# A mixture-of-experts layer: 64 of 256 tokens by gathered rows on VectorE, the down tiles as plain fp32 products, no weight table

## The chip, the core and the metric

One core of a Trainium2 chip runs the whole program in one launch. The metric is the device time in microseconds, from the first to the last work of the program. One execution with the hardware profiler on gives the trace.

## The reference

One decoder layer on 256 tokens of 1024 features: a mixing part (retention and sparse attention) and then PEER, a mixture of 16384 single-neuron experts, in which each token picks 16 experts in each of 8 heads. The change is in the PEER part:

```python
q = (hblk @ w_q).reshape(B, TB, PEER_HEADS, 2, PEER_DHALF)
s = jnp.einsum('btphd,phnd->btphn', q, subkeys).astype(jnp.float32)
v, i = lax.top_k(s, PEER_TOPK)
cand = (v[..., 0, :, None] + v[..., 1, None, :]).reshape(B, TB, PEER_HEADS, PEER_TOPK * PEER_TOPK)
cidx = (i[..., 0, :, None] * PEER_NKEYS + i[..., 1, None, :]).reshape(...)
tv, tj = lax.top_k(cand, PEER_TOPK)
eidx = jnp.take_along_axis(cidx, tj, axis=-1)
w = jax.nn.softmax(tv, axis=-1)
u = w_down[eidx]
a = jax.nn.gelu(jnp.einsum('btd,btpkd->btpk', hblk, u).astype(jnp.float32))
vv = w_up[eidx]
return jnp.einsum('btpk,btpkd->btd', (w * a).astype(hblk.dtype), vv)
```

After it come a gated residual add and a final RMSNorm. `w_down` and `w_up` are 16384 x 1024 in float32, 64 MB each.

## The kernel before

**Stages.** Up to 182 us runs the part before PEER ("prefix"). Then a list of units is worked off in order: 16 `wq` units (the query products, 512 KB of weights each), 128 `down` units and 128 `up` units. A unit takes one tile of 128 experts, 512 KB, all 256 tokens at once, so all 16384 experts are computed densely. Down tile n: the 256 tokens' h2 times 128 rows of `w_down`, then Gelu, kept as a 128 x 256 tile of V (tiles 0 to 63 in `VL`, the others in `VH`). Up tile j: V's tile j times 128 rows of `w_up`, added up in four banks of PSUM (`acc_o[tt][hf]`: two halves of the tokens, two halves of the features). V holds Gelu values times routing weights, and these are zero for the experts that a token did not pick.

**How a product is made.** TensorE takes float32 in a fast form, fp32r, that keeps fewer bits. So every streamed tile `raw` is split into a high part `H` (ScalarE, a copy into fp32r) and a rest `L` (VectorE, raw minus H), and a product is three: high x high, rest x high, high x rest (`mm3`). In the rows, `hH,H`, `hL,H` and `hH,L` are those of a down tile (8 chunks of 128 features x 3 = 24 products of 256 columns), and `H,a`, `L,a`, `H,a` those of an up tile (4 banks x 3 = 12 products of 512 columns), where `a` is V's tile split the same way (`a1`, `a2`).

**Selection.** Beside the wq units and the first downs, VectorE picks the top 16 of each half and head (`top_gen`). The generator is stepped by a credit per unit (`CQ`, `CT`), each step naming its price.

**Routing weights.** They are put in place in two ways. Tokens 0 to 127 by one-hots (`w_gen`): for 4 tokens at a time VectorE and ScalarE make one-hot matrices of the two halves of the expert numbers (`o`, `ow`, f16), and 8 small products give the 128 x 128 weights of each token, which are multiplied into V (or copied there, and the Gelu multiplied in later as `g`). This makes 32 groups between down units, one for each unit at the price `CD`. Tokens 128 to 255 by a table in DRAM, `wd`: GpSimd writes zeros into it (8 transfers of 1 MB), then adds the weights with 128 scattered transfers (`put_weights`, line 1009), and each up unit loads its 128 x 128 part `wt2` (64 KB, in the rows `wt<-wd`), which VectorE multiplies into V's tile in `up_units`.

**Order of units.** Ups begin when `w_gen` is done and `START_UP` units have passed: then the downs that are left alternate with ups, and the rest are ups alone. Tiles are loaded on SP's queue `PRE = 4` units ahead, into `RAW = 3` raw buffers; the split of a unit is issued one unit ahead (`SPL`), with `HB = LB = 4` buffers. Each engine works off its own queue of instructions in order. `gate_unit` (8 products of 128 x 1024 on VectorE with the gate's weights `wadaT`) is put to every fourth up from `GATE`. The last three up units are one block, in which a bank is finished before the next is begun, and the tail (gate, residual, norm, store) follows.

Of the kernel before, what the change touches and what calls it, by code (L numbers as in the profile page):

```python
# [24 lines left out]
F32 = mybir.dt.float32  # L25
# [11 lines left out]
P = 128  # L37
T = 256
# [13 lines left out]
GATE = 28  # L52
# [5 lines left out]
ZC = 2048  # L58
START_UP = 108
# [6 lines left out]
def build(tc, I, out, dbg=None, stop=None):  # L66
# [60 lines left out]
    wd2 = mk(dpool, (NT * P, P), F32, "wd")  # L127
    wd = wd2.rearrange("a (b o) -> (a b) o", o=1)
# [13 lines left out]
    def split(key, n=None):  # L142
# [3 lines left out]
        S.activation(h[:, :n], r[:, :n], AF.Copy)  # L146
# [43 lines left out]

    pre = ExitStack()
# [116 lines left out]
    hH = mk(pers, (P, KC, T), F32R, "hH")  # L308
    hL = mk(pers, (P, KC, T), F32R, "hL")
# [83 lines left out]
    dump("hT", f(hH))  # L393
# [401 lines left out]
    h2H = mk(pers, (P, KC, T), F32R, "hH")  # L795
    h2L = mk(pers, (P, KC, T), F32R, "hL")
    ss2 = mk(pp, (P, 2, 3), F32, "ss2")
    shift = [mod[:, 3 * KC + k:3 * KC + k + 1] for k in range(KC)]
    for tt in range(2):
# [26 lines left out]
        for hf, b in enumerate(bs):  # L826
# [8 lines left out]
            for q in range(4):  # L835
# [12 lines left out]
    if stop == "prefix":  # L848
        Q.dma_start(out[0:P, :], f(h2H).rearrange("p a b -> p (a b)")[:, :D])
        psp["es"].close()  # L850
        es.close()
        return

# [75 lines left out]
    def top_gen(sc):  # L929
# [8 lines left out]
        for tt in (1, 0):  # L938
# [40 lines left out]
            if tt:  # L979
                continue  # L980
# [386 lines left out]
```

## Time and profile before

| | |
|---|---|
| Median of 3 runs | 1027.58 us (1026.66 to 1028.56) |
| The profiled execution | 1026.25 us |
| Its span, first to last instruction | 1024.4 us |
| TensorE / VectorE / ScalarE / GpSimd busy | 990.2 / 742.9 / 558.2 / 271.1 us |
| Mean granted TensorE clock | 0.993 |
| First wq product / start of the last matmul | 182.05 / 1013.56 us |
| Wq units | 182 to 236 us |
| Downs with selection beside them | 236 to 386 us |
| 32 weight groups between downs | 386 to 526 us |
| Downs alone | 526 to 590 us |
| 16 pairs of a down and an up | 590 to 682.7 us |
| 109 ups alone | 682.7 to 1003 us |
| Last three ups, then the tail | to 1013.9 us, to 1024.4 us |

An engine's busy time is the union of its instructions. Matmuls overlap in the rows (a product of 256 columns shows 0.28 us, but the next starts 0.12 us later), so the price of a product is read from one start to the next. A wait stands in the "idle before" column of a group, with what released it. In the rows an operation stands at the line of a helper, L82, so they are told apart by tile.

### The profile page before, as it was taken

What the parts mean: (1) busy time and instruction counts of PE and PEld (TensorE: products, weight loads), DVE (VectorE), ACT (ScalarE), POOL (GpSimd) and SP (SyncE); (2) the same over time, 40 slices, a digit from 0 to 9 for tenths busy, and PEclk for the clock granted to TensorE, in tenths of its full rate; (3) what the DMA queues carried; (4) which work ended last, traced back from release to release, by engine and by line L of the source; (5) the groups of instructions that cost most, each with busy time, mean ns of one, the idle gap of its engine ahead of it and who ended that gap; (6) DMA issues with size and microseconds to landing.
All of it is one profiled execution on the core that took longest, in us unless ns stands there. A gap on an engine that the chain in (4) does not pass through costs nothing. (4 is left out here: it accounts for less than half of the span.)

```text
span 1024.4 us, 17290 instructions
## 1 busy us (share of the span) xinstructions
PE 990.2 (97%) x6323; PEld 870.8 (85%) x6323; DVE 742.9 (73%) x1647; ACT 558.2 (54%) x1077; POOL 271.1 (26%) x175
## 2 busy tenths in 40 slices
PE   7999999999999999999999999999999989999995
PEld 6876678999999999999999979988877668777773
DVE  7987988899999997667755455656666656655656
ACT  7544984455544548777754454554444445444443
POOL 1040000200087787787778600000000000000001
PEclk9999999999999999999999999999999999999998
DMA  9979654975577776666676567766778776666662
GB/s 367 409 298 342 209 196 128 356 297 181 175 181 188 183 178 153 142 146 142 139 157 184 134 211 208 206 203 195 251 242 252 244 246 208 200 201 201 205 194 81
DMA packets 94196, 216.00 MB, mean 211 GB/s; under 512 B 27912, under 2 KB 44576, under 8 KB 92704
## 3 DMA queue, kind: packets, MB, share of 16 engines
q1 hardware_dynamic: 73632, 201.99, 61.2%
q0 software_dynamic: 20336, 12.66, 7.6%
q8 instruction: 49, 0.80, 0.3%
q14 instruction: 35, 0.29, 0.1%
q10 hardware_dynamic: 144, 0.26, 0.1%
HBM read 204.31 MB, written 10.56 MB: 210 GB/s over the span
## 5 line engine op out<-in xcount | busy, mean ns | idle before, releaser
L82 ACT ACTIVATE H<-raw 128x1024 fp32r<-128x1024 f32 x284 | 300.2, 1059 | 246.9 <-DMA raw<-in_up_dram 138.2
L82 DVE TENSOR_TENSOR L<-raw,H 128x1024 fp32r<-128x1024 f32 x284 | 346.0, 1219 | 57.1 <-ACT H L82 53.4
L82 PE MATMUL acc<-H,a 128*128 128x512 f32 (+1 forms) x1030 | 325.4, 394 | 8.9 <-DVE a L82 5.7
L1009 POOL DMA_INDIRECT wd<-VL x128 | 241.0, 1883 | 151.1 <-DVE VL L82 95.9
L82 PEld LDWEIGHTS acc<-H,a 128*128 128x128 f32 x1030 | 190.9, 189 | 56.0 <-DVE a L82 10.6
L82 PE MATMUL acc<-L,a 128*128 128x512 f32 (+1 forms) x515 | 203.4, 395 | 6.1 <-DVE L L82 5.7
L82 PE MATMUL acc<-hH,H 128*128 128x256 f32 x704 | 201.8, 287 | 0.0
L82 PE MATMUL acc<-hL,H 128*128 128x256 f32 x704 | 199.6, 284 | 0.0
L82 PE MATMUL acc<-hH,L 128*128 128x256 f32 x704 | 199.2, 283 | 0.0
L82 PEld LDWEIGHTS acc<-hL,H 128*128 128x128 f32 x704 | 134.6, 191 | 0.2 <-DVE hL L82 0.2
L82 PEld LDWEIGHTS acc<-hH,H 128*128 128x128 f32 x704 | 134.6, 192 | 0.0
L82 PEld LDWEIGHTS acc<-hH,L 128*128 128x128 f32 x704 | 134.5, 191 | 0.0
L82 PE MATMUL dn<-hH,H 128*128 128x256 f32 x448 | 127.6, 285 | 0.0
L82 PE MATMUL dn<-hH,L 128*128 128x256 f32 x448 | 126.8, 283 | 0.6 <-DVE L L82 0.6
L82 PE MATMUL dn<-hL,H 128*128 128x256 f32 x448 | 126.8, 283 | 0.0
L82 PEld LDWEIGHTS acc<-L,a 128*128 128x128 f32 x515 | 97.1, 188 | 33.8 <-DVE L L82 14.7
L82 PEld LDWEIGHTS dn<-hH,H 128*128 128x128 f32 x448 | 85.8, 191 | 0.6
L82 PEld LDWEIGHTS dn<-hH,L 128*128 128x128 f32 x448 | 85.6, 191 | 0.8 <-DVE L L82 0.8
L82 PEld LDWEIGHTS dn<-hL,H 128*128 128x128 f32 x448 | 85.6, 191 | 0.6
L82 DVE TENSOR_TENSOR VL<-VL,wt 128x128 f32<-128x128 f32 x64 | 18.6, 291 | 85.5 <-DMA wt<-wd 85.5
L82 DVE TENSOR_TENSOR VH<-VH,wt 128x128 f32<-128x128 f32 x64 | 18.7, 292 | 74.4 <-DMA wt<-wd 74.4
L82 ACT ACTIVATE ow<-o,VL 128x128 f16<-128x128 f16 x128 | 52.4, 578 | 0.0
(345 smaller groups left out, 1212.5 us busy)
## 6 DMA issues: line engine op xcount, KB each, us to landing
raw<-in_down_dram SPq DMA_DIRECT2D x128, 512.0 KB, 3.8
raw<-in_up_dram SPq DMA_DIRECT2D x128, 512.0 KB, 4.0
adaraw<-in_wadaT_dram SPq DMA_DIRECT2D x40, 512.0 KB, 7.0
raw<-in_wq_dram SPq DMA_DIRECT2D x16, 512.0 KB, 8.3
wd<-VL POOLq DMA_DIRECT2D x8, 1024.0 KB, 18.2
wt<-wd SPq DMA_DIRECT2D x128, 64.0 KB, 3.3
raw<-in_win_C_dram SPq DMA_DIRECT2D x12, 512.0 KB, 7.4
rawA<-in_win_A_dram SPq DMA_DIRECT2D x8, 512.0 KB
```

The source lines that it names most:

```text
L82: i = fn(*a, **kw)
L1009: i = G.indirect_dma_start(wd, bass.IndirectOffsetOnAxis(ap=eid[:, p, k:k + 1], axis=0), exd[:, p, k:k + 1], None, compute_op=ALU.add)
```

## The change

The tokens are divided anew: 64 sparse ones (`TS`, tokens 0 to 63) and 192 dense ones (`TD`).

- The sparse tokens go without dense tiles. Each has 128 picked experts; two tokens' lists lie over the 128 partitions in halves (`idxS`, `wS`: partition p is token p of the first 64 slots, partition 64 + p the same token's other 64). 64 gathers of 128 rows of `downN` (512 KB each, on GpSimd's queue) bring the rows, and VectorE multiplies each with the token's own h2 (`h2rep`) and sums over the features into a column of `dotS`; Gelu and weight give `cS`; then 64 gathers of rows of `up` follow, which VectorE adds up, scaled, into `accS`. The rows have `BD + 1 = 4` buffers. A step (one gathered tile) is issued by a credit of 0.7 for each down and 0.45 for each up unit.
- The dense down tiles are plain fp32 products of the raw tile with `h2f` (192 columns), 8 a tile, with no split.
- The up tiles take 10 products instead of 12: the 64 dense tokens of the first half go as 128 columns, high and rest side by side, with two products for each half of the features; the other 128 tokens as before. `a` is made one unit ahead (`prepare`).
- All 192 dense tokens get their weights by one-hots (48 groups); table, zeroing, scattered additions and `wt2` are gone. Ups begin as soon as the groups are done.
- The halves of the packed columns and of `accS` are brought together in the last block by 8 products with a matrix `sel`.
- `RAW` is 4, `HB` and `LB` 3. The gate's weights are loaded one gate step earlier.

The diff, cut to its core:

```diff
-RAW = 3
-HB = 4
-LB = 4
+RAW = 4
+HB = 3
+LB = 3
-GATE = 28
+GATE = 36
+TS = 64
+TD = T - TS
+NJ = P // 2
+BLK = 8
+BD = 3
+RD = 0.7
+RU = 0.45
-START_UP = 108
...
+    for hf in range(2):
+        b = bank("S")
+        for q in range(4):
+            k = hf * 4 + q
+            for n, a in enumerate((h2H, h2L)):
+                mm(b[:, q * P:(q + 1) * P], a[:, k, :P], identR, n == 0, n == 1)
+        S.activation(h2rep[:TS, hf * 512:(hf + 1) * 512], b[:TS, :], AF.Copy)
+    G.dma_start(h2rep[TS:, :], h2rep[:TS, :])
+    for n in range(2):
+        G.tensor_tensor(h2f[:, 4 * n:4 * n + 4, :], h2[n][:, :, 0, TS:].bitcast(F32), h2[n][:, :, 1, TS:].bitcast(F32),
+                        op=ALU.add)
...
+    def gather(tag, src, j, bufs):
+        r = mk(sp, (P, D), F32, tag, bufs=bufs)
+        G.indirect_dma_start(r, None, src, bass.IndirectOffsetOnAxis(ap=idxS[:, j:j + 1], axis=0))
+        return r
...
+        get_d(BD)
+        yield
+        for j in range(NJ):
+            r = rowD.pop(j)
+            V.scalar_tensor_tensor(r, r, 1.0, h2rep, op0=ALU.mult, op1=ALU.mult, accum_out=dotS[:, j:j + 1])
+            get_d(j + 1 + BD)
+            if j + 1 + BD > NJ:
+                get_u(j + 1 + BD - NJ)
+            if j % BLK == BLK - 1:
+                js = slice(j + 1 - BLK, j + 1)
+                S.activation(cS[:, js], dotS[:, js], AF.Gelu_apprx_tanh)
+                V.tensor_tensor(cS[:, js], cS[:, js], wS[:, js], op=ALU.mult)
+            yield
+        for j in range(NJ):
+            V.scalar_tensor_tensor(accS, rowU.pop(j), cS[:, j:j + 1], accS, op0=ALU.mult, op1=ALU.add)
+            get_u(j + 1 + BD)
+            yield
...
     def down_unit(n):
-        h, l = splits.pop(("down", n))
+        r, _ = raws.pop(("down", n))
...
-            mm3(b, h[:, ks], l[:, ks], h2H[:, k, :], h2L[:, k, :], k == 0, k == KC - 1)
+            mm(b, r[:, k * P:(k + 1) * P], h2f[:, k, :], k == 0, k == KC - 1)
...
+    def prepare(j, ap):
...
+            a = mk(ap, (P, TD, 2), F32R, "a", bufs=3)
+            S.activation(a[:, :, 0], v, AF.Copy)
+            last["U"] = V.tensor_tensor(a[:, :, 1], v, f(a[:, :, 0]), op=ALU.subtract)
...
     def up_units(js, ap):
...
-            V.tensor_tensor(v[:, P:], v[:, P:], wts.pop(j), op=ALU.mult)
...
+                        if tt:
+                            pr = ((a[:, TS:, 0], h), (a[:, TS:, 0], l), (a[:, TS:, 1], h))
+                        else:
+                            a0 = a[:, :TS, :].rearrange("p a b -> p (a b)")
+                            pr = ((a0, h), (a0, l))
...
+        if spg:
+            scred += RU if u == "up" else RD
+            while scred >= 1.0 and spg:
+                scred -= 1.0
+                with tc.issue_after(last["U"].ins):
+                    if next(spg[0], StopIteration) is StopIteration:
+                        spg.pop()
```

On TensorE, before, the end of a down tile and the first up tile behind it (`dn` and `acc` are PSUM banks; 24 rows of the first kind make a tile, 12 of the second):

```order
L82 MATMUL dn_7689<-hH_1712,H_7650 128x256
L82 MATMUL dn_7689<-hL_1713,H_7650 128x256
L82 MATMUL dn_7689<-hH_1712,L_7651 128x256
L82 MATMUL acc_7570<-H_7685,a_1357_7727 128x512
L82 MATMUL acc_7570<-L_7686,a_1357_7727 128x512
L82 MATMUL acc_7570<-H_7685,a_1358_7728 128x512
L82 MATMUL acc_7571<-H_7685,a_1357_7727 128x512
L82 MATMUL acc_7571<-L_7686,a_1357_7727 128x512
L82 MATMUL acc_7571<-H_7685,a_1358_7728 128x512
```

After, the last downs alone and the first up tile; a row with x8 is a whole down tile:

```order
L87 MATMUL dn_5885<-h2f_1960,raw_5799 128x192 x8
L87 MATMUL acc_5822<-H_5881,a_5899 128x512
L87 MATMUL acc_5822<-L_5882,a_5899 128x512
L87 MATMUL acc_5823<-H_5881,a_5899 128x512
L87 MATMUL acc_5823<-L_5882,a_5899 128x512
L87 MATMUL acc_5824<-H_5881,a_5899 128x512
L87 MATMUL acc_5824<-L_5882,a_5899 128x512
L87 MATMUL acc_5824<-H_5881,a_5899 128x512
L87 MATMUL acc_5825<-H_5881,a_5899 128x512
L87 MATMUL acc_5825<-L_5882,a_5899 128x512
L87 MATMUL acc_5825<-H_5881,a_5899 128x512
```

A down tile has become 8 products of 192 columns with the raw tile itself as the stationary one, and each of the first two banks of an up tile has lost its third product.

On VectorE, before, in the middle of the ups alone:

```order
L82 TENSOR_TENSOR a_1614_9023<-VL_1953,a_1613_9022 128x256
L82 TENSOR_TENSOR VL_1953<-VL_1953,wt_1598_8959 128x128
L82 TENSOR_TENSOR L_9018<-raw_8932,H_9017 128x1024
L82 TENSOR_TENSOR a_1620_9048<-VL_1953,a_1619_9047 128x256
L82 TENSOR_TENSOR VL_1953<-VL_1953,wt_1604_8984 128x128
L82 TENSOR_TENSOR L_9043<-raw_8957,H_9042 128x1024
L82 TENSOR_TENSOR a_1626_9073<-VL_1953,a_1625_9072 128x256
```

After, at a like place:

```order
L87 SCALAR_TENSOR_TENSOR accS_2003<-row_8147,cS_2002,accS_2003 128x1024
L87 TENSOR_TENSOR L_8275<-raw_8209,H_8274 128x1024
L87 TENSOR_TENSOR a_8278<-VH_3713,a_8278 128x192
L87 TENSOR_TENSOR L_8294<-raw_8231,H_8293 128x1024
L87 TENSOR_TENSOR a_8297<-VH_3713,a_8297 128x192
L87 TENSOR_TENSOR L_8313<-raw_8250,H_8312 128x1024
L87 TENSOR_TENSOR a_8316<-VH_3713,a_8316 128x192
L87 SCALAR_TENSOR_TENSOR accS_2003<-row_8188,cS_2002,accS_2003 128x1024
```

The product with `wt` is gone, `a` has 192 columns instead of 256, and a step of `accS` stands behind every second or third tile.

On GpSimd, before, from the spill of x2 on:

```order
L842 DMA x2d_71<-xn_92 128x2048
L877 DMA subT_1960<-in_subT_dram 128x2048
L878 IOTA ioi_1961 128x512
L879 IOTA tok_1962 128x1
L884 MEMSET VL_1953 128x2048
L886 DMA wd_74<-VL_1953 128x2048 x8
L1009 DMA wd_74<-VL_1953 2097152x1 x128
```

After, from the same place (a row of 128 x 1024 is one gather):

```order
L872 DMA x2d_71<-xn_94 128x2048
L899 DMA subT_1989<-in_subT_dram 128x2048
L869 TENSOR_TENSOR h2f_1960<-hT_417_1714 128x768
L869 TENSOR_TENSOR h2f_1960<-hT_418_1715 128x768
L900 IOTA ioi_1990 128x512
L866 DMA h2rep_1938<-h2rep_1938 64x1024
L996 DMA idxS_1999<-ei_3232 64x64
L997 DMA wS_2000<-ex_3225 64x64
L1032 MEMSET accS_2003 128x1024
L1024 DMA row_3268<-in_downN_dram,idxS_1999 128x1024
```

Zeroing and scattered additions have made way for the sum `h2f`, two copies into the lower partitions and 128 gathers, each behind the row step that frees its buffer.

## Rows read from the trace of the kernel before

**Rows 1.** The page, busy time of each engine, its share of the span, instructions.

```profile
PE 990.2 (97%) x6323; PEld 870.8 (85%) x6323; DVE 742.9 (73%) x1647; ACT 558.2 (54%) x1077; POOL 271.1 (26%) x175
```

**Rows 2.** Busy us by stretch: stretch, its length, engines, TensorE clock, DMA share, GB/s.

```profile
236.00:386.00 150.00, 150.00 (x1253) 150.00 (x1252) 145.02 (x361) 76.92 (x113) 85.01 (x44) 1.00 0.70 182
386.00:526.00 140.00, 139.92 (x1171) 137.97 (x1171) 94.91 (x218) 108.53 (x283) 109.09 (x65) 1.00 0.65 145
...
590.00:682.70 92.70, 90.18 (x575) 81.59 (x575) 54.48 (x89) 46.93 (x85) 0.00 (x0) 1.00 0.69 205
682.70:1003.00 320.30, 309.12 (x1313) 243.86 (x1311) 198.12 (x340) 149.23 (x218) 2.25 (x5) 0.99 0.70 220
1003.00:1013.90 10.90, 9.52 (x45) 7.04 (x45) 9.02 (x13) 5.31 (x10) 2.59 (x2) 1.00 0.01 4
1013.90:1024.40 10.50, 0.00 (x0) 0.00 (x0) 6.11 (x18) 3.34 (x10) 1.27 (x1) 0.65 0.27 100
```

**Rows 3.** Timeline of TensorE: start us, length us, engine, line, operation, out<-in, count.

```profile
400.32 1.11 PE L82 MATMUL w<-ow,o 128*128 128x128 f16 x8
...
401.39 0.28 PE L82 MATMUL dn<-hL,H 128*128 128x256 f32 x1
...
601.27 0.28 PE L82 MATMUL dn<-hH,H 128*128 128x256 f32 x1
...
604.15 0.40 PE L82 MATMUL acc<-H,a 128*128 128x512 f32 x1
...
606.89 0.28 PE L82 MATMUL dn<-hH,H 128*128 128x256 f32 x1
```

**Rows 4.** The page, the chain that ended last, share of the span by line.

```profile
DMA wt<-wd 23%; POOL wd L1009 4%; PE acc L82 4%; PE dn L82 4%; DVE L L82 2%; DVE VL L82 2%; DVE VH L82 2%; DMA VL<-in_wadaT_dram 2%; DMA raw<-in_up_dram 1%; DVE a L82 1%; DMA raw<-in_down_dram 0%; ACT H L82 0%; DMA wd<-VL 0%; ACT VL L82 0%; SPq L82 0%
```

**Rows 5.** Lines, 683 to 1003 us: groups, count, busy, mean ns, idle before, releasers.

```profile
L82 DVE TENSOR_TENSOR L<-raw,H 128x1024 fp32r<-128x1024 f32 x107 | 130.4, 1219 | 2.2 <-ACT H L82 2.0
L82 ACT ACTIVATE H<-raw 128x1024 fp32r<-128x1024 f32 x108 | 114.5, 1060 | 149.3 <-DMA raw<-in_up_dram 138.2 <-PE acc L82 7.8 <-PE dn L82 1.6
...
L82 DVE TENSOR_TENSOR a<-VH,a 128x256 fp32r<-128x256 f32 x62 | 26.0, 419 | 0.7 <-ACT a L82 0.5
...
L82 DVE TENSOR_TENSOR VH<-VH,wt 128x128 f32<-128x128 f32 x63 | 18.4, 292 | 73.9 <-DMA wt<-wd 73.9
```

**Rows 6.** DMA, 683 to 1003 us: issues with KB and median us to landing.

```profile
DMA packets 32813, 70.33 MB, mean 220 GB/s; under 512 B 3785, under 2 KB 17543, under 8 KB 32666
...
raw<-in_up_dram SPq DMA_DIRECT2D x107, 512.0 KB, 4.0
```

**Rows 7.** DMA, 26 to 51 us.

```profile
DMA packets 3078, 10.23 MB, mean 409 GB/s; under 512 B 341, under 2 KB 341, under 8 KB 3076
...
raw<-in_win_C_dram SPq DMA_DIRECT2D x4, 512.0 KB, 7.4
```

**Rows 8.** Timeline of TensorE, fp32 products.

```profile
208.06 0.61 PE L82 MATMUL w<-subT,qTi 128*128 128x128 f32 x4
...
208.63 0.28 PE L82 MATMUL acc<-hL,H 128*128 128x256 f32 x1
...
87.66 5.37 PE L82 MATMUL O<-praw,blk 128*30 128x256 f32 x24
92.95 1.12 PE L82 MATMUL S<-keys,qT 128*128 128x512 f32 x2
```

**Rows 9.** Timeline of VectorE.

```profile
21.30 1.22 DVE L82 SCALAR_TENSOR_TENSOR adaraw<-adaraw,cs 128x1024 f32<-128x1024 f32 x1
```

**Rows 10.** Lines, GpSimd, 300 to 400 us.

```profile
L1009 POOL DMA_INDIRECT wd<-VL x40 | 78.5, 1962 | 24.1 <-issue 11.3 <-DVE oe L82 5.0 <-DVE L L82 4.4
```

**Rows 11.** Busy us of the same stretch, columns as in the stretches above.

```profile
300.00:400.00 100.00, 99.92 (x834) 99.56 (x834) 93.67 (x198) 55.83 (x99) 76.21 (x40) 1.00 0.71 175
```

**Rows 12.** The page, DMA issues: count, KB each, median us to landing.

```profile
wd<-VL POOLq DMA_DIRECT2D x8, 1024.0 KB, 18.2
```

**Rows 13.** The tile wd: durations in ns, least, median, greatest.

```profile
L1009 POOL DMA_INDIRECT wd<-VL x128: 1549/1666/2948, 279.1 to 580.6; - x128
```

More of the change, by code (lines that the diff above doesn't have):

```diff
@@ L306, in x_copy, with __init__, __getitem__ @@
         S.activation(xT[:, 2 * i:2 * i + 2, :], b, AF.Copy)
-    hH = mk(pers, (P, KC, T), F32R, "hH")
-    hL = mk(pers, (P, KC, T), F32R, "hL")
+    class Parts:
+        def __init__(self, tiles, n):
+            self.tiles, self.n = tiles, n
+        def __getitem__(self, at):
+            _, k, c = at
+            if isinstance(k, slice):
+                return self.tiles[k.start // 4][:, :, self.n, c]
+            return self.tiles[k // 4][:, k % 4, self.n, c]
+    hT2 = [mk(pers, (P, 4, 2, T), F32R, f"hT{n}") for n in range(2)]
+    hH, hL = Parts(hT2, 0), Parts(hT2, 1)
     pq = [bank("S"), bank("S")]
@@ L847, in build @@
     pre.close()
[L848 to L852, printed above, removed]
     psum_pool("ps3")
@@ L937, in top_gen @@
                 yield 1.1
-        for tt in (1, 0):
+        for tt in range(2):
             fi = mk(tk, (P, 8, 2, 16), F32, "fi", bufs=2)
@@ L1000, in top_gen @@
             yield 1.0
-    sync = mybir.DependencyInfo(mybir.DependencyClass.Sync, mybir.DependencyReason.DATA)
-    placed = []
-    def put_weights(p):
-        group = []
-        for k in range(16):
-            i = G.indirect_dma_start(wd, bass.IndirectOffsetOnAxis(ap=eid[:, p, k:k + 1], axis=0),
-                                     exd[:, p, k:k + 1], None, compute_op=ALU.add)
-            for o in group:
-                tc.declare_no_dep(i.ins, o.ins, reason="a head's places all differ")
-            for o in placed:
-                tc.add_manual_dep(i.ins, o.ins.name, sync, reason="the head before has been added")
-            group.append(i)
-        placed[:] = group
+    idxS = mk(sp, (P, NJ), I32, "idxS")
@@ new lines, in build, with sparse_gen, get_d, get_u @@
+    wS = mk(sp, (P, NJ), F32, "wS")
+    dotS = mk(sp, (P, NJ), F32, "dotS")
+    cS = mk(sp, (P, NJ), F32, "cS")
+    accS = mk(sp, (P, D), F32, "accS")
+    spg = []
+    def gather(tag, src, j, bufs):
+        r = mk(sp, (P, D), F32, tag, bufs=bufs)
+        G.indirect_dma_start(r, None, src, bass.IndirectOffsetOnAxis(ap=idxS[:, j:j + 1], axis=0))
+        return r
+    def sparse_gen():
+        downN = I["downN"]
+        upN = I["up"].rearrange("a b c -> (a b) c")
+        with tc.issue_after(last["G"].ins):
+            G.memset(accS, 0.0)
+        rowD, rowU = {}, {}
+        nd, nu = [0], [0]
+        def get_d(n):
+            while nd[0] < min(n, NJ):
+                rowD[nd[0]] = gather("row", downN, nd[0], BD + 1)
+                nd[0] += 1
+        def get_u(n):
+            while nu[0] < min(n, NJ):
+                rowU[nu[0]] = gather("row", upN, nu[0], BD + 1)
+                nu[0] += 1
+        get_d(BD)
[15 more added lines that the diff above has]
+            yield
@@ L1018, in w_gen @@
     def w_gen(ohp):
         half = NT // 2
-        for gi in range(P // 4):
-            t0 = gi * 4
+        for gi in range(TD // 4):
+            v0 = gi * 4
+            t0 = TS + v0
             oh = []
@@ L1159, in build @@
     credit = 0.0
+    scred = 0.0
     qs = []
@@ L1178, in build @@
         elif u == "up":
+            prepare(n, apool)
+            nxt = next((m for w, m in seq[i + 1:] if w == "up"), None)
+            if nxt is not None:
+                prepare(nxt, apool)
             up_units([n], apool)
```

169 lines of the change are left out of this document (90 added, 79 removed).

## The prediction

> **What bounds the kernel now.** I read the page's busy times first. TensorE is busy 97% of the span and VectorE 73% [rows 1], so TensorE's own work is the first thing to count, and its gaps the second. The stretches show where the gaps are [rows 2]: from 236 to 526 us TensorE is busy for all but 0.1 of 290 us, so there only fewer or cheaper matmuls shorten the program. From 682.7 to 1003 us it is busy 309.1 of 320.3 us. That is the stretch with only up tiles, and its busy time flatters it, because the ends of matmuls are modelled. So I went to the timeline of TensorE. An up tile is 12 products of 512 columns, 604.15 to 606.89 us, 2.74 us or 0.228 each [rows 3]. With 0.227 the 109 tiles of the stretch need 109 x 12 x 0.227 = 296.9 us; 23.4 of the 320.3 us are waits. By the same count the 16 pairs of a down and an up tile before it lose about 3 us (92.7 against 16 x 5.61) and the last three up tiles 2.7 (10.9 against 36 x 0.227). So 29 us of waits lie in the up phase and next to none before.
>
> Who is waited for there? The chain that ended last gives 23% of the span to the arrival of `wt`, the 64 KB piece of the weight table [rows 4]. In the up-only stretch ScalarE's H waits 138 us for the raw up tile and VectorE's product with half of the values 74 us for `wt` [rows 5]. VectorE works in order, so an L (the low half of the next tile) that stands behind a product waiting for `wt` is late, and TensorE with it. The loads there land 4.0 us after issue, with three raw buffers, at 220 GB/s [rows 6], when the same queue moved 409 GB/s from 26 to 51 us [rows 7]. So it is the round trip of a few buffers that binds, not bandwidth.
>
> **The change part by part.** The sum is made against the profiled execution's 1026.25 us; the median of the runs is 1.3 above it.
>
> *Down tiles as plain fp32.* Now 24 products of 256 columns, 601.27 to 604.15 us: 2.88 us [rows 3]. After: 8 fp32 products of 192 columns. No such product is in the trace; the nearest rows are fp32 of 128 columns and of 256 columns, which are counted twice, as two passes. The four passes of 128 columns and one ordinary product of 0.12 fill 208.06 to 208.63 us, so a pass takes (0.57 - 0.12) / 4 = 0.112; 24 passes of 256 columns take 87.66 to 92.95 us, 0.220 each [rows 8]. Half way between them, 192 columns cost 0.166, and 16 passes 2.65 us. Bounds: three quarters of the 256-column pass gives 2.64; with 1.5 times the 128-column pass it is 2.70; and if a pass carries the fixed part that the ordinary products show (0.120 for 256 and 0.228 for 512 columns leave 0.012 each, so 0.161 + 0.012 = 0.173) 2.77. I take 2.65: 128 x (2.88 - 2.65) = **-29** (-31 to -14). The split of the down tiles goes too, 128 each of H (1.06 us) and L (1.22 us) [rows 5], off TensorE's path in the stretches where it waits for nobody.
>
> *Up tiles of 10 products instead of 12.* 125 x 2 x 0.227 = **-57**. Six of the ten take every second column of `a` as stationary. The f16 products of the weight groups read with a stride of the same 8 bytes and fit 8 into 0.95 us, 0.12 each [rows 3], under 0.227, so loading the stationary tile stays covered; cover gone would mean more than 0.227 for one load, which no row shows.
>
> *16 more weight groups* (48 for 32). A group starts at 400.32 us and the second ordinary product behind it at 401.39; less one 0.12 it is 0.95 us [rows 3]: 16 x 0.95 = **+15**. VectorE's and ScalarE's part of a group lies beside TensorE, since the 386 to 526 stretch has them at 95 and 109 of 140 us, with the splits of the down tiles still in it [rows 2].
>
> *No table.* The 8 zeroing transfers, 128 scattered additions and 128 `wt` reloads go, and the product with `wt` on VectorE. This takes away the wait that ends last in the up phase. Also, `a` is prepared one unit ahead and raw buffers are four. All 29 us of waits would go if nothing is late next. What is late next is VectorE: per up unit it now has L 1.22, `a` of three quarters of 0.42, and 0.45 of a row step. A row step is a 128x1024 scalar-tensor-tensor, 1.22 us in the row of 21.30 us [rows 9]. That is 1.22 + 0.31 + 0.55 = 2.08 of the 2.27 us of a unit (10 x 0.227), 92%. In the 32 units that hold the eight gate steps it is 0.30 more, 2.38: over the unit by 0.11, 4 us in all. DMA: 1.45 x 0.524 MB in 2.27 us is 335 GB/s, 82% of the 409 that were seen [rows 7]. I leave 10 us of waits (bounds 0 and the 29 of now): **-19**.
>
> *The gathers.* 128 of 512 KB, 67 MB more, on GpSimd's queue. Issue: the scattered additions took 1.96 us each on GpSimd between 300 and 400 us, with VectorE 94% busy [rows 10, 11]. A step comes each 2.65 / 0.7 = 3.8 us in the down phase and each 2.27 / 0.45 = 5.0 us among the ups, so issue fits. Gather j+3 is issued after step j, so its round trip has three periods, 11 to 15 us. Nearest rows: the 512 KB loads of SP land in 4.0 us [rows 6], in the saturated stretch in 7.4 [rows 7]; GpSimd's 1 MB writes in 18.2 [rows 12]. I take 5 to 9 us, no wait; 18.2 is kept for the rivals. Queued behind a waiting row step on VectorE are L and `a`, for which TensorE waits.
>
> Against these gathers speaks the Trainium skill, "SBUF — State Buffer", Who interferes with whom: while VectorE holds the port that it shares with GpSimd, GpSimd can't write the descriptors of its own queue's transfers. The trace disagrees in the one place that it shows: 40 issues took 78.5 us within a window in which VectorE was idle for 6.3 [rows 10, 11]. By that rule the sum would be the third rival below.
>
> *Smaller.* Last three tiles: 30 products and 8 for the merge instead of 36, **+0.4**. `h2rep`, 16 products of 128 columns at about 0.066 (half of 256 columns and the fixed part) before the first wq unit, **+1**. The tail: merging the first 64 tokens comes late in the last unit, **+2** of the 10.5 us after the last matmul [rows 2]. Selection (top): VectorE was busy 145 of 150 us from 236 to 386 [rows 2] with some 52 L in it (150 / 2.88; 63 us) that go, against 13 row steps (16 us) that come: **0**. `h2f` on GpSimd and the copies of indices: hidden, GpSimd is idle there but for them.
>
> Sum: -29 - 57 + 15 - 19 + 0.4 + 1 + 2 = -86.6. Own time 1026.25 - 86.6 = 939.7; median **941 us**.
>
> **The rivals.**
> 1. *All waits go*, no 10 us left and no late tail: 941 - 12 = 929, with the lowest price of the down tiles 927. For it: bandwidth is at 82%. Against: VectorE at 92% and in-order.
> 2. *The loads become the bound.* With the gathers beside them a load's landing goes from 4.0 to the 7.4 of the saturated stretch [rows 6, 7]. A raw buffer is then held 7.4 + 1.06 + 1.22 and, with a guess of 0.7 for the handing on, 10.4 us, over four buffers 2.6 us a unit instead of 2.27: 109 x 0.33 = 36, less the 10 of waits that I have already, +26; with the weight stage's share +30: 967 to 971. For it: H waits for loads 138 us already at 220 GB/s [rows 5, 6]. Against: demand is 335, not 409.
> 3. *Descriptors only in VectorE's pauses.* VectorE leaves 0.2 us in a unit of 2.27, and 0.45 of an issue of 1.55 us (the shortest of the scattered additions [rows 13]) needs 0.70: 0.5 us more a unit, 125 x 0.5 = +62, less the 10 counted already: 993. Against: the 40 issues of 1.96 us beside a busy VectorE [rows 10, 11].
> 4. *The other side, slower: the gathers' round trip.* With three periods in flight the step takes a third of the round trip R once that is longer than the pace. The pace of 64 steps is 3.8 and of 64 is 5.0; the loss 64 (R/3 - 3.8) + 64 (R/3 - 5.0) eats the 86.6 us at R/3 = 5.08, R = 15.2 us. At 18.2 us, the landing of GpSimd's 1 MB writes [rows 12], the loss is 213 us and the time 1154. For it: that one row. Against: it is a write of twice the bytes, eight at once; the loads are far under it.
> 5. *The change doesn't do what it says*: a plain fp32 pass is no cheaper, 2.77 to 2.88 us a tile: 956 to 970.
>
> **How the numbers follow.** Forecast 0.55, rival 1 0.13, rival 2 0.19, rival 3 0.03, rival 4 0.05, rival 5 0.05. The likeliest gives 941 (own range 932 to 955). From 915 to 980 are the forecast, rivals 1, 2 and 5, with something below rival 1 for a lighter prefix; I count 0.85 of them in. Less than 0.2% either way is what a measurement of this kernel can't tell from no change. Faster: all but rival 4 and a mild form between: 0.92; same 0.02; slower 0.06.
>
> **What would show it.** Right: down tiles of 16 passes in 2.6 to 2.7 us; ten products of 0.227 in an up unit; up-only stretch near 2.3 us a unit, its waits shared by L and H; the weight stage with 0.95 us a group; no waits of row steps above 1 us; last matmul about 13 us before the end. Wrong: landing of raw tiles at 7 us or more (rival 2), GpSimd issues above 2.5 us (rival 3), VectorE waiting for `row` (rival 4), or a pass of 192 columns above 0.17 us. A clock below 0.99 in the up phase would make every product dearer and is in none of the terms; now it is 0.99 to 1.00 there [rows 2].

## The result and the profile after

The changed kernel takes 970.71 us (968.37 to 974.82, 4 runs), the kernel before 1027.12 us beside it; the ratio is 0.9443, 95% interval 0.9412 to 0.9474. That is 56 us less where 86.6 had been forecast: inside the range, at the time that rival 2 gave, and, as the experiments show, only partly for rival 2's reason. The profiled execution has a span of 969.0 us (1024.4 before).

The page's busy times of the changed kernel answer to [rows 1]:

```profile
PE 919.9 (95%) x5198; PEld 816.2 (84%) x5198; DVE 731.3 (75%) x1668; ACT 456.0 (47%) x1031; POOL 195.1 (20%) x172
```

The stretches, as in [rows 2]: the part before PEER, wq units, downs with the selection, weight groups, pairs of a down and an up, ups alone, last block, tail. Columns: stretch, its length, busy us of TensorE, its loads, VectorE, ScalarE, GpSimd, TensorE's clock, DMA share, GB/s.

```profile
0.00:190.60 190.60, 179.51 (x1014) 136.77 (x1014) 155.89 (x345) 112.98 (x252) 17.49 (x30) 1.00 0.73 265
190.60:243.40 52.80, 52.80 (x448) 52.80 (x447) 48.08 (x226) 23.24 (x45) 4.73 (x4) 1.00 0.46 150
243.40:377.40 134.00, 125.48 (x764) 125.12 (x763) 94.54 (x334) 25.74 (x69) 22.20 (x22) 0.96 0.76 255
377.40:571.00 193.60, 193.60 (x1299) 190.80 (x1297) 127.47 (x353) 107.64 (x363) 36.23 (x38) 1.00 0.77 257
...
583.80:689.30 105.50, 96.11 (x496) 84.98 (x496) 59.81 (x88) 31.99 (x59) 24.03 (x20) 1.00 0.87 306
689.30:948.60 259.30, 252.53 (x1074) 207.14 (x1074) 223.13 (x280) 142.90 (x216) 80.86 (x52) 0.99 0.92 336
...
956.00:969.00 13.00, 0.00 (x0) 0.00 (x0) 8.03 (x21) 4.09 (x12) 4.36 (x3) 0.70 0.22 82
```

Three of these are off. The part before PEER ends at 190.6 us and ended at 182; in the selection TensorE has 8.5 us without work and a mean clock of 0.96; and the pairs and the ups alone still have TensorE idle for some 16 us by busy time, at 306 and 336 GB/s.

The timeline of TensorE, answering to [rows 3]: a down tile between two weight groups, then ten products of an up tile.

```profile
378.35 2.78 PE L87 MATMUL dn<-h2f,raw 128*128 128x192 f32 x16
380.97 1.10 PE L87 MATMUL w<-ow,o 128*128 128x128 f16 x8
381.89 0.51 PE L87 MATMUL acc<-h2f,raw 128*128 128x192 f32 x2
```

```profile
860.63 0.39 PE L87 MATMUL acc<-H,a 128*128 128x512 f32 x1
...
862.95 0.40 PE L87 MATMUL acc<-H,a 128*128 128x512 f32 x1
```

A down tile takes 380.97 - 378.35 = 2.62 us, a weight group 0.92, both as forecast (2.65, 0.95). The ten products of an up tile take 862.95 - 860.63 = 2.32 us, 0.232 each, not 0.227.

The chain that ended last, as in [rows 4], now goes mostly through TensorE itself, and through the raw up tiles where it went through `wt`:

```profile
PE acc L87 34%; DMA raw<-in_up_dram 12%; PE dn L87 12%; PE w L87 6%; PE C L87 5%; PE O L87 4%; PE S L87 3%; DVE L L87 2%; PE T L87 2%; ACT H L87 1%; DMA VL<-csd 1%; DVE accS L87 1%; DVE row L87 1%; DMA row<-in_downN_dram,idxS 1%; DMA VL<-in_wadaT_dram 1%
```

The groups of lines of the ups alone, as in [rows 5], and the transfers there, as in [rows 6]:

```profile
L87 DVE TENSOR_TENSOR L<-raw,H 128x1024 fp32r<-128x1024 f32 x107 | 130.8, 1222 | 28.0 <-ACT H L87 27.5
...
L87 ACT ACTIVATE H<-raw 128x1024 fp32r<-128x1024 f32 x107 | 113.6, 1062 | 118.7 <-PE acc L87 50.6 <-DMA raw<-in_up_dram 47.8 <-DVE L L87 20.0
...
L1024 POOL DMA_INDIRECT row<-in_up_dram,idxS x47 | 77.9, 1658 | 163.5 <-DVE accS L87 149.9 <-DVE a L87 13.1 <-DVE L L87 0.3
L87 DVE SCALAR_TENSOR_TENSOR accS<-row,cS,accS 128x1024 f32<-128x1024 f32 x51 | 65.2, 1278 | 0.0
```

```profile
raw<-in_up_dram SPq DMA_DIRECT2D x104, 512.0 KB, 6.3
...
row<-in_up_dram,idxS POOLq DMA_INDIRECT x47, 8.2
```

H waits less for loads (47.8 us for 138), but a raw tile lands in 6.3 us instead of 4.0, and a gathered tile in 8.2. No row step waits for its gather here: the accS group has no idle time before it.

Who keeps TensorE waiting is told by the waits (waiting engine, line, what for: us in total, times, longest). First the pairs, then the ups alone:

```profile
ACT H L87 <- DMA raw<-in_up_dram: 54.2, 18, 4.5
...
PE dn L87 <- ACT g L87: 8.5, 8, 1.3
```

```profile
PE acc L87 <- DVE a L87: 6.6, 2, 3.8
DVE VL L87 <- DMA VL<-in_wadaT_dram: 4.8, 1, 4.8
DVE VL L87 <- DMA VL<-csd: 3.1, 1, 3.1
```

In the pairs TensorE waits for a bank that ScalarE has yet to empty (`g`), and `g` stands in ScalarE's queue behind an H whose raw up tile is late. In the ups alone the list has no wait of TensorE for L or H. Its two waits, 2.8 us up to 741.5 us and 3.8 us up to 800.4, are for `a`, which stands on VectorE behind a gate step that waited for its own load: first `csd`, then a piece of `wadaT`. Behind both, some ten products start up to 0.43 us apart instead of 0.232, at a granted clock of 0.64 and 0.57. So the two cost 4.8 and 5.6 us. Between them TensorE worked without a gap, beside 367 GB/s:

```profile
746.20:796.20 50.00, 50.00 (x217) 41.37 (x216) 45.13 (x59) 27.21 (x42) 17.50 (x10) 1.00 0.98 367
```

### The profile page after: what moved, and what is told of

Same layout as the page of the kernel before. It is cut to its first block, busy times and chain, and to the rows that moved or that the text cites. A ratio compares the mean times of both kernels' runs of the same rounds, so it can differ in the third digit from the quotient of the medians.

```text
span 969.0 us, 14801 instructions
## 1 busy us (share of the span) xinstructions
PE 919.9 (95%) x5198; PEld 816.2 (84%) x5198; DVE 731.3 (75%) x1668; ACT 456.0 (47%) x1031; POOL 195.1 (20%) x172
## 4 chain that ended last, share of the span: by engine, by line
PE 65%; DMA 16%; DVE 10%; issue 4%; ACT 3%; POOL 1%; SPq 0%; DVEq 0%; ACTq 0%; POOLq 0%
PE acc L87 34%; DMA raw<-in_up_dram 12%; PE dn L87 12%; PE w L87 6%; PE C L87 5%; PE O L87 4%; PE S L87 3%; DVE L L87 2%; PE T L87 2%; ACT H L87 1%; DMA VL<-csd 1%; DVE accS L87 1%; DVE row L87 1%; DMA row<-in_downN_dram,idxS 1%; DMA VL<-in_wadaT_dram 1%
## 5 line engine op out<-in xcount | busy, mean ns | idle before, releaser
L87 ACT ACTIVATE H<-raw 128x1024 fp32r<-128x1024 f32 x156 | 165.1, 1061 | 196.0 <-DMA raw<-in_up_dram 102.6
L87 DVE TENSOR_TENSOR L<-raw,H 128x1024 fp32r<-128x1024 f32 x156 | 190.2, 1221 | 70.1 <-ACT H L87 69.0
L87 PE MATMUL acc<-h2f,raw 128*128 128x192 f32 x1120 | 191.3, 326 | 0.0
L87 PEld LDWEIGHTS acc<-h2f,raw 128*128 128x128 f32 x1120 | 182.3, 191 | 0.0
L87 PE MATMUL dn<-h2f,raw 128*128 128x192 f32 x928 | 162.9, 330 | 17.1 <-ACT VL L87 8.5
L87 PEld LDWEIGHTS dn<-h2f,raw 128*128 128x128 f32 x928 | 153.5, 192 | 22.2 <-ACT g L87 12.5
L1024 POOL DMA_INDIRECT row<-in_up_dram,idxS x64 | 98.1, 1533 | 224.8 <-DVE accS L87 158.2
L1024 POOL DMA_INDIRECT row<-in_downN_dram,idxS x64 | 65.2, 1019 | 252.4 <-DVE row L87 216.2
L87 DVE SCALAR_TENSOR_TENSOR row<-row,h2rep 128x1024 f32<-128x1024 f32 x64 | 78.0, 1219 | 10.8 <-DMA row<-in_downN_dram,idxS 10.8
L87 DVE SCALAR_TENSOR_TENSOR accS<-row,cS,accS 128x1024 f32<-128x1024 f32 x64 | 81.9, 1279 | 3.7 <-DMA row<-in_up_dram,idxS 3.6
L87 PE MATMUL acc<-hT,H 128*128 128x256 f32 x256 | 47.8, 287 | 0.0
```

The source lines that it names most:

```text
L87: i = fn(*a, **kw)
L1024: G.indirect_dma_start(r, None, src, bass.IndirectOffsetOnAxis(ap=idxS[:, j:j + 1], axis=0))
```

## The experiments

The stretches of each run are cut at the same events: first wq product, last score, first and last weight group, first up, last down, last product.

**No row step beside the selection.** What TensorE waits for at 327 us in the changed kernel stands in its timeline and in that of ScalarE. First TensorE (in square brackets the wait before a row and its releaser), then ScalarE:

```profile
322.17 5.36 PE L87 MATMUL acc<-h2f,raw 128*128 128x192 f32 x32
336.05 4.80 PE L87 MATMUL dn<-h2f,raw 128*128 128x192 f32 x16 [8.52 <-ACT VL L87]
340.69 4.55 PE L87 MATMUL acc<-h2f,raw 128*128 128x192 f32 x27
```

```profile
332.75 1.28 ACT L87 ACT_TABLE_LOAD   x1 [23.39 <-DVE ex L87]
```

TensorE waits 8.5 us for ScalarE to empty a bank (VL), and ScalarE stands 23.4 us at the exp of the selection (with its table load), waiting for VectorE's `ex`. The Gelus of finished down tiles are queued behind that exp. Ahead of `ex`, VectorE had row steps:

```profile
L87 DVE SCALAR_TENSOR_TENSOR row<-row,h2rep 128x1024 f32<-128x1024 f32 x14 | 17.1, 1221 | 5.7 <-DMA row<-in_downN_dram,idxS 5.7
```

14 steps, 17.1 us, and 5.7 us of waits for their gathers; 12 of the steps and all of the waits lie ahead of `ex`. Behind the wait of TensorE 16 passes take 340.69 - 336.05 = 4.64 us where they take 2.62 elsewhere; the granted clock is 0.57 there.

```diff
-RD = 0.7
+RD = 0.88
...
-        if spg:
+        if spg and phase != "top":
             scred += RU if u == "up" else RD
```

> No row step while the selection runs; the 128 steps are spread over the rest (0.88 a down, 0.45 an up). Theory: the 8.5 us that TensorE waits at 327 us for a bank come from ScalarE's exp of the selection, which waits for VectorE, late by the row steps beside the selection; the slow 3.4 us behind the wait are a consequence. Then the stretch from the first down to the first weight group goes from 134 to about 123 us, the time from 970.7 to about 960. Rival: VectorE is late there by the selection alone (its code puts the one-hots of a head behind that head's top 16 now); then a wait of 6 to 9 us stays and the time is 968 to 972.

Measured: 967.79 us (962.08 to 970.08; ratio 0.9422, interval 0.9379 to 0.9465). The theory's 960 was not reached, and the time alone doesn't tell it from the change; the stretch does (the profiled execution is the fastest of the four):

```profile
244.20:366.90 122.70, 122.70 (x760) 122.61 (x759) 76.56 (x298) 24.94 (x66) 6.79 (x7) 1.00 0.67 214
573.20:682.60 109.40, 97.35 (x496) 86.21 (x495) 66.42 (x100) 33.33 (x61) 31.29 (x27) 0.99 0.90 318
```

From the last score to the first group it is 122.7 us with no idle time, against 133.4. So the row steps, with their gathers, make the wait, and the rival falls. Part of it may have come back: the pairs, with 0.88 steps a down instead of 0.7, took 109.4 us where the change took 105.5, and 106.8 in a second profile.

**Transfers or VectorE in the up phase.** Two kernels part the load of the gathers on the DMA engines from that of the row steps on VectorE. In the first, the 64 gathers of `up` rows are left out:

```diff
-                rowU[nu[0]] = gather("row", upN, nu[0], BD + 1)
+                rowU[nu[0]] = h2rep
```

> The 64 gathers of rows of up are left out: VectorE's accS steps read h2rep instead of a gathered row, so the sparse tokens' sum is not the layer's; VectorE's work is the same, 33 MB of transfers are missing. Theory (transfers): the raw up tiles land in 4.0 to 4.5 us instead of 6.3, the up-only stretch falls from 2.45 to 2.30 to 2.35 us a unit and the pairs from 5.55 to about 5.0, together 20 to 25 us: 946 to 951. Rival (VectorE's row steps delay L): VectorE has the same to do, the time stays 966 to 972.

In the second, each step does a sixteenth of its columns:

```diff
-            V.scalar_tensor_tensor(accS, rowU.pop(j), cS[:, j:j + 1], accS, op0=ALU.mult, op1=ALU.add)
+            V.scalar_tensor_tensor(accS[:, :64], rowU.pop(j)[:, :64], cS[:, j:j + 1], accS[:, :64], op0=ALU.mult,
+                                   op1=ALU.add)
```

> The gathers stay whole, but each accS step works on 64 of the 1024 columns, so the sparse tokens' sum is only partly made; a step is about 0.15 instead of 1.28 us. Theory (transfers): landing stays above 6 us, the time falls by at most 5 us, 965 to 971. Rival (VectorE): 64 x 1.1 us of VectorE go, the waits of the up phase with them, 15 to 25 us: 946 to 956.

Measured: 954.91 us (952.95 to 955.22) without the gathers, 973.90 (971.69 to 975.28) with short steps. Pairs and ups alone, first without gathers, then with short steps:

```profile
584.20:680.90 96.70, 94.53 (x495) 85.43 (x494) 60.05 (x88) 33.13 (x60) 3.85 (x3) 1.00 0.75 244
680.90:939.70 258.80, 255.56 (x1111) 210.90 (x1109) 228.53 (x288) 145.81 (x221) 2.85 (x5) 1.00 0.74 240
```

```profile
584.00:686.80 102.80, 96.55 (x495) 84.62 (x494) 46.58 (x88) 32.83 (x60) 20.96 (x21) 1.00 0.89 316
686.80:956.70 269.90, 260.19 (x1111) 212.53 (x1109) 182.88 (x288) 145.95 (x222) 53.16 (x53) 0.99 0.88 321
```

With VectorE's work kept (60.1 + 228.5 us) but 240 GB/s, the two stretches take 355.5 us; with VectorE lighter by 59 us (46.6 + 182.9) and about 320 GB/s, 372.7; in the change they took 105.5 + 266.4 = 371.9 by the same cuts. So the gathers' transfers make 16.4 us of the waits, less than the 20 to 25 that were expected: 8.8 in the pairs, and 7.6 in the ups alone, where the gate's wait for `csd` falls from 3.1 to 0.3 us (the one for `wadaT`, 4.5 us, stays, and TensorE's 2.9 us behind it).

The kernel with short steps lies above both of its expected ranges and can't price VectorE's steps in the ups alone: VectorE waits 18.2 us for the gate's loads there, where it waited 4.8, and TensorE 9.5 us for `a`. That the steps cost nothing there rests on the change's own trace, in which TensorE has no wait for L in the ups alone. In the pairs VectorE's share may be 2 to 3 us (105.5 to 102.8), not much more than two profiles of the change differ by (105.5 and 106.8 us; 266.4 and 268.5 for the ups alone).

**The buffer counts, alone on the kernel before.** The change sets RAW 4 and HB and LB 3. With these on the kernel before, the order of TensorE's instructions ahead of the wq units is row for row that of the changed kernel (names of the two halves of h aside):

```diff
-RAW = 3
-HB = 4
-LB = 4
+RAW = 4
+HB = 3
+LB = 3
```

> The kernel before with the buffer counts of the change (RAW 4, HB and LB 3) and nothing else. Theory: these counts alone reorder the instructions ahead of the wq units, and cost there what the change lost: the first wq product comes at 187 to 191 us instead of 182; with nothing gained later 1032 to 1036, and if a fourth raw buffer takes waits out of the up phase down to 1020. Rival: the 8 us are chance of one profile or of the new operand layout; then the first wq product stays at 181 to 183 us.

Measured: 1022.76 us (1020.19 to 1027.66; ratio 0.9955, interval 0.993 to 0.998). The first wq product starts at 189.6 us, where it was 182.1; and from the last down to the last product it is 318.7 us where it was 330.9.

```profile
0.00:189.60 189.60, 176.70 (x999) 133.72 (x999) 155.05 (x342) 111.67 (x249) 17.89 (x30) 0.99 0.73 265
691.80:1010.50 318.70, 309.76 (x1357) 253.06 (x1355) 207.38 (x352) 155.36 (x228) 5.02 (x7) 0.99 0.73 221
```

So of the 8.6 us that the change lost ahead of the wq units, 7.5 are the reordering that these counts bring about, in code that the diff doesn't touch; and the same counts had 12 of the 29 us of waits, without any other part of the change.

**The stride of the stationary tiles.** The up products cost 0.232 us now. The split values were laid one behind the other:

```diff
-            a = mk(ap, (P, TD, 2), F32R, "a", bufs=3)
-            S.activation(a[:, :, 0], v, AF.Copy)
-            last["U"] = V.tensor_tensor(a[:, :, 1], v, f(a[:, :, 0]), op=ALU.subtract)
+            a = mk(ap, (P, 2 * TD), F32R, "a", bufs=3)
+            S.activation(a[:, P:P + TS], v[:, :TS], AF.Copy)
+            S.activation(a[:, :P], v[:, TS:], AF.Copy)
+            V.tensor_tensor(a[:, P + TS:2 * P], v[:, :TS], f(a[:, P:P + TS]), op=ALU.subtract)
+            last["U"] = V.tensor_tensor(a[:, 2 * P:], v[:, TS:], f(a[:, :P]), op=ALU.subtract)
```

> The split values of an up tile lie one behind the other (high of the later 128 tokens, high and rest of the first 64, rest of the later 128) instead of high and rest alternating, so that every stationary tile of an up product is read without a stride; one instruction more on ScalarE and one on VectorE for each tile. Theory: the stride is why an up product of 512 columns now takes 0.232 us and took 0.227 in the kernel before; then it is 0.227 again and 1250 x 0.005 = 6 us go: 962 to 967. Rival: the stationary load is covered and the 0.232 have another cause; pitch 0.232 and 968 to 974.

Measured: 969.00 us (963.23 to 971.12; ratio 0.9406, interval 0.9372 to 0.944). Ten products in its timeline:

```profile
806.12 0.39 PE L87 MATMUL acc<-H,a 128*128 128x512 f32 x1
...
808.46 0.39 PE L87 MATMUL acc<-H,a 128*128 128x512 f32 x1
```

2.34 us: no better than 2.32. But another tile of the same trace takes 2.27:

```profile
889.01 0.39 PE L87 MATMUL acc<-H,a 128*128 128x512 f32 x1
...
891.28 0.39 PE L87 MATMUL acc<-H,a 128*128 128x512 f32 x1
```

With contiguous values both kinds occur: of 96 stretches of ten products without a wait, 36 take less than 2.275 us and 45 more than 2.325. In the change no ten products in a row take less than 2.28. Over all products without a wait the mean from one start to the next is 0.2302 us here, 0.2319 in the change and 0.2279 in the kernel before. So the stride has a part in it, some 0.002 of 0.004 us a product or 2 us in all, which the time can't show; what makes the slow tiles that are left stays open. It isn't the traffic alone (without the gathers, at 240 GB/s, the mean is 0.2317), nor three H buffers as such (the kernel before with HB 3 has 0.2275).

**More steps early.** The steps were moved into the weight stage:

```diff
-RD = 0.7
-RU = 0.45
+RD = 1.4
+RU = 0.3
...
-            scred += RU if u == "up" else RD
+            scred += RD if phase == "w" else RU if u == "up" else 0.0
```

> No row step during the selection, 1.4 a down while the weight groups run and in the downs behind them, none at the downs of the pairs and 0.3 an up. Theory: TensorE's wait for ScalarE's exp goes (the stretch from the first down to the first group 134 to 123), and with a third fewer gathers beside the ups the pairs lose 5 to 8 us less and the ups alone 5 to 8; the weight stage has VectorE at some 178 of 193 us and transfers near 370 GB/s, and stays at 193: 943 to 953. Rival: the weight stage becomes bound by transfers or VectorE and grows by 10 us or more: 957 to 970.

Measured: 966.27 us (965.27 to 968.13; ratio 0.9399, interval 0.9372 to 0.9427): in the rival's range, but neither theory alone. The selection lost its wait (122.6 us) and the pairs are down to 94.6, but the weight stage grew by 9.4 us at 350 GB/s (95% of the DMA engines' time), and the end got longer. The stretches:

```profile
366.20:569.00 202.80, 199.18 (x1317) 195.07 (x1315) 172.25 (x423) 104.79 (x368) 90.75 (x79) 0.99 0.95 350
578.80:673.40 94.60, 94.05 (x496) 85.45 (x495) 43.93 (x67) 34.67 (x59) 6.68 (x6) 1.00 0.75 250
```

The waits of the weight stage (waiting engine, line, what for: us in total, times, longest):

```profile
DVE row L87 <- DMA row<-in_downN_dram,idxS: 11.5, 12, 1.9
...
PE w L87 <- DVE ow L87: 3.0, 3, 2.1
```

Row steps wait for their gathers, and TensorE's weight groups for VectorE's `ow` behind them: rival 4's wait, at last, in a small way. The end of TensorE's work:

```profile
940.66 0.28 PE L87 MATMUL acc<-H,a 128*128 128x256 f32 x1
945.12 0.74 PE L87 MATMUL w<-row,sel 128*128 128x512 f32 x2 [4.19 <-ACT row L87]
946.38 2.92 PE L87 MATMUL w<-row,sel 128*128 128x512 f32 x6 [0.52 <-DVE row L87]
```

At 0.3 an up the steps had not come to their end, some eight were left over for the last block, and the merge (`sel`) began 4.5 us and ended 8 us after the last up product instead of ahead of it. That was a mistake of the experiment's rates, and it shows what its forecast left out: the merge needs the last step before it.

**The downs as three products again.** The part of the change that I had counted for 29 us was undone (with three row buffers instead of four, for space):

```diff
-        r, _ = raws.pop(("down", n))
+        h, l = splits.pop(("down", n))
...
-            mm(b, r[:, k * P:(k + 1) * P], h2f[:, k, :], k == 0, k == KC - 1)
+            ks = slice(k * P, (k + 1) * P)
+            mm3(b, h[:, ks], l[:, ks], h2H[:, k, TS:], h2L[:, k, TS:], k == 0, k == KC - 1)
```

> The downs as three fp32r products of 192 columns with the split on ScalarE and VectorE again, the rest as in the change (one row buffer fewer, for space). Theory A: an fp32r product of 192 columns costs its columns and the fixed part, 0.093 us (between 0.120 for 256 and half of that), 2.2 us a tile instead of 2.62, and TensorE would gain 50 us, but VectorE, with 1.22 us more a tile, binds selection and the weight stage: 950 to 975. Theory B: loads of the stationary tile can't come closer than 0.12 us; then a tile stays at 2.9 us, and with VectorE's load the time is 1000 to 1020.

Measured: 1052.95 us (1050.3 to 1054.03; ratio 1.023, interval 1.0194 to 1.0265), 24 us above the kernel before beside it. A tile of 24 products in its timeline, then the selection, and TensorE's largest wait in it (us in total, times, longest):

```profile
250.92 0.39 PE L87 MATMUL acc<-hT,H 128*128 128x192 f32 x2
...
253.60 0.39 PE L87 MATMUL acc<-hT,H 128*128 128x192 f32 x2
```

```profile
243.10:432.20 189.10, 145.12 (x1134) 141.38 (x1132) 163.35 (x390) 70.40 (x114) 22.84 (x21) 0.88 0.56 179
```

```profile
PE acc L87 <- DVE L L87: 22.2, 13, 6.5
```

A tile takes 253.60 - 250.92 = 2.68 us, 0.112 a product: nearer theory B, since an fp32r product of 192 columns costs hardly less than one of 256 (0.120). But the 82 us over the change, more than either theory gave, are not there (128 x 0.06 = 8). Most lie in the selection: with the split of the downs back on VectorE and the row steps beside it, it takes 189 us instead of 133, TensorE waits 42 us for L (22.2, and 19.8 for the downs in `dn`), and its clock is 0.88 on the mean. What of it belongs to the split and what to the one row buffer fewer was not parted: the row steps wait 18.1 us for their gathers there, where they wait 5.7 in the change.

**A version from these findings.** The contiguous split values, no steps beside the selection, 1.2 a down in the weight stage, none at the downs and 0.3 at the ups of the pairs, 0.53 at the ups alone, so that the steps end before the last block; and the same with a fourth H buffer. The change itself ran once more beside them.

```diff
-RD = 0.7
-RU = 0.45
+RD = 1.2
+RU = 0.53
+RM = 0.3
...
-        if spg:
-            scred += RU if u == "up" else RD
+        if spg and phase != "top":
+            pairs = any(w == "down" for w, _ in seq[i:])
+            scred += RD if phase == "w" else 0.0 if u == "down" else RM if pairs else RU
```

> The contiguous split values, no row step during the selection, 1.2 a down while the weight groups run, none at the downs and 0.3 at the ups of the pairs, 0.53 at the ups alone, so that the last step ends some seven units before the end. By the stretches seen so far: selection 123 us (134 in the change), weight stage 193 to 199, pairs 95 to 98 (105.5), ups alone 258 to 264 (266), merge on time: 970 - 11 + 3 - 9 - 4 = 949, range 944 to 957. If a lighter load in one stretch only comes back in another, as the sum of transfers is the same, it is 958 to 966.

```diff
-HB = 3
+HB = 4
```

> As the kernel with spread steps, with four H buffers instead of three. Theory: buffer counts decide the order ahead of the wq units, so the first wq product moves again, to anywhere from 182 to 192 us (the order is neither that of before nor that of the change); a fourth H lets ScalarE run one tile ahead and takes 2 to 6 us out of the up phase: 940 to 958. Rival: the first wq product stays within 1 us of 190.5 and nothing changes: 947 to 951.

> The change itself once more, on the chip of the two others, so that they can be compared: 968 to 973, first wq product at 190 to 191 us, the wait of 8 to 9 us in the selection again.

Measured, on one chip: 947.23 us (945.3 to 948.13; ratio 0.9262, interval 0.9242 to 0.9282), 942.99 us (942.31 to 945.92; ratio 0.923, interval 0.9209 to 0.9252), and the change 974.13 us (966.41 to 977.28; ratio 0.9507, interval 0.9471 to 0.9543). So the two beat the change by 27 and 31 us. The change shows its waits again: the first wq product at 190.9 us, and 9.2 us in the selection. The spread steps, selection, weight stage and pairs; then the part before PEER with four H buffers:

```profile
244.30:367.00 122.70, 122.70 (x760) 122.61 (x760) 76.66 (x298) 24.95 (x66) 6.80 (x7) 1.00 0.67 215
367.00:560.20 193.20, 193.20 (x1296) 190.49 (x1295) 158.90 (x412) 106.95 (x369) 73.45 (x67) 1.00 0.90 330
573.20:667.60 94.40, 93.28 (x496) 84.92 (x495) 45.54 (x83) 35.69 (x78) 4.73 (x5) 1.00 0.74 252
```

```profile
0.00:187.90 187.90, 177.93 (x1015) 135.17 (x1015) 155.51 (x345) 113.77 (x253) 17.64 (x30) 0.99 0.74 269
```

Against the change on this chip the first version's gain lies in the selection (122.6 us for 135.1) and the pairs (94.4 for 106.8); from the last down to the last product it is 264.7 for 268.5. At 330 GB/s the weight stage is free of waits (193.2 of 193.2 us), at 350 it was not. With four H buffers the order ahead of the wq units is a third one, and the first wq product stands at 187.9 us instead of 190.9: 3 of the 4 us between the two.

## Why the prediction was right in direction and 30 us off

By its terms, in the profiled executions:

- **Down tiles**: 2.62 us for 2.65, so -33 for -29. Right, and the interpolation between passes of 128 and 256 columns held (0.163 for 0.166). What I costed at nothing, that the splits leave VectorE, weighed more here: with the splits back at the same rates of row steps, and one row buffer fewer, the kernel is 82 us slower, and TensorE's own price is 8 of them. With the steps elsewhere it was not tried.
- **Up tiles**: two products of twelve went, but the other ten cost 0.232: 125 x (2.74 - 2.32) = -52 for -57. I had held the load of a strided stationary tile to be covered, from f16 products; with the stride gone a part of the tiles were back at 2.27 us, so it has a part, and the rest is open.
- **Weight groups**: 16 x 0.92 = +15, as forecast. The whole weight stage ran without a wait.
- **The waits of the up phase**: forecast 10 of the 29 us left. With 2.62 and 2.32 as prices, the 19 pairs lose 105.5 - 19 x 4.94 = 11.6 us, and from the last down to the last product it is 266.4 - 106 x 2.32 - 38 x 0.23 = 11.7: 23 us left, -6 for -19. This is the step that failed in the argument and not only in size: I named VectorE (92% by my sum) as what is late next. Loads were, and what stands behind them in a queue that is worked off in order: in the pairs the raw up tiles, with ScalarE's `g` behind H; in the ups alone two loads of the gate, with `a` behind them on VectorE, 10.4 of the 11.7 us with the half clock that follows. I had counted the gate steps' work (4 us) and put their loads at nothing. The raw tiles' landing, 6.3 us for 4.0, made TensorE wait in the pairs alone.
- **Selection, forecast 0**: +10.7 us. The busy sum was right (VectorE had less to do than before), and beside the point. The exp of the selection stands in ScalarE's queue ahead of the Gelus, and the row steps ahead of its input, with 5.7 us of gather waits, made that late. I listed L and `a` as what is queued behind a row step, and forgot ScalarE's exp, with the banks of TensorE behind it. One of my signs of being right fails here as well: the first row step waited 3.15 us for its gather, where none was to wait above 1.
- **Ahead of the wq units, forecast +1**: +8.6, of which 7.5 are the buffer counts, and 1.1 `h2rep`. I had taken the order there as given.
- **Last block and tail**: 13.3 us after the start of the last product for 10.8: +2.5 for +2.

Together -33 - 52 + 15 - 6 + 11 + 9 + 2.5 = -53.5, against the measured -55.4; the wq units are 1 us shorter. That the time lies inside the range is owed in part to its width: the 19 us ahead of the wq units and in the selection stand in the sum as +1 and 0 and in no rival, and fell where the range was kept open for rival 2.

Of the rivals: 1 fell; 2 held in the pairs, and not in the ups alone, where it had its price of 36 us: no wait of TensorE for a raw tile stands there (the waits of the whole up phase are 13 us more than the forecast's 10, where it had 26 to 30). That the time came out at its 971 is chance; 3 held in a mild form that costs nothing: the gathers' issue on GpSimd is longer where VectorE is busier (1.66 us a gather in the group of rows above, against a least value of 0.94), but GpSimd is idle for 163 us there, so no step is late. 4 fell: gathers land in 8.2 us where 15 would decide. 5 fell. On their chip the last versions take 74 and 79 us off the kernel before (1021.63 us there), against the 86.6 of the forecast: most of what it gave to the parts is there, once the row steps stand elsewhere. That the gain of 27 to 31 us over the change is about the 30 that the prediction was off says no more, since 9 and 6 us are still lost ahead of the wq units.

## What to carry to other kernels

A busy share below one doesn't say that an added instruction is free: look for the one instruction with a due time that stands behind it, on the other engines' queues too, and for what is queued behind that. A mean rate of transfers doesn't say whether one load is on time: here 50 us at 367 GB/s ran without a wait and 306 GB/s did not. Look for the load that an in-order queue stands still for and for what stands behind it, and put extra transfers into the stretch that has least. Buffer counts of a shared pool are an edit to every stage that uses the pool, so look at the order of the stages that the diff doesn't name.

## What the runs showed of the hardware

- An fp32r product of 192 columns took 0.112 us where one of 256 takes 0.120 and one of 512 takes 0.227 (0.232 in the change): 192 columns saved hardly anything over 256. Those of 128 columns that make `h2rep` took 0.11 too, not the 0.066 of the prediction. A plain fp32 pass of 192 columns took 0.163.
- After 8.5 us without work, TensorE took 4.64 us for 16 passes that take 2.62 at the full clock, at a granted clock of 0.57 (1 is 2.4 GHz, one half 1.2). After 2.8 and 3.8 us in the ups alone most of the next ten products started 0.43 us apart instead of 0.232, at 0.64 and 0.57. The run whose selection waits again and again has 0.88 over that stretch.
- The issue of a gather on GpSimd depends on what VectorE does. In the ups alone it took 1.66 us on the mean in the change and, with row steps of 64 columns, 1.09:

```profile
L1024 POOL DMA_INDIRECT row<-in_up_dram,idxS x47 | 51.4, 1093 | 185.1 <-DVE accS L87 168.8 <-DVE L L87 7.3 <-DVE a L87 7.1
```

The Trainium skill, "SBUF — State Buffer", Who interferes with whom, has a VectorE instruction with two SBUF inputs contend with a GpSimd instruction that reads SBUF, and keeps the full lock for VectorE's 2-port modes, a limit that the prediction left out. The row step has two such inputs and the gather reads `idxS`, so the direction agrees with these two numbers; the issue is stretched and not shut out.
- Beside the weight groups, 330 GB/s cost TensorE nothing; at 350 GB/s, with VectorE 13 us busier, the stretch was 9.4 us longer and VectorE waited for gathers. The Trainium skill, "DMA: Bandwidth & Descriptors", Specifications, gives about 358 GB/s as a core's share of HBM; 409 GB/s were seen in this case ([rows 7]), so it is no ceiling here. Nor does the mean rate tell whether a load is late: raw tiles were in the pairs, at 306 GB/s, and TensorE had no wait over 50 us at 367.
